# Gates and the first norm's sums by quarters of the tokens in column groups, in place of a gate tile and one running sum

## The chip, the cores and the metric

The kernel runs on one core of a Trainium2 chip. The metric is device time in microseconds, the median of the runs shown. TensorE (PE in the profile) multiplies, VectorE (DVE), ScalarE (ACT) and GpSimd (POOL) do the elementwise work, and SyncE (SP) issues nearly all transfers.

## The reference, cut to what matters

One layer of a hybrid decoder: 576 tokens (512 of a prompt, 64 samples), model width 2048. What this change touches is the first norm, the gates taken from its output, and the softplus and sigmoid of those gates.

```python
h = _rmsnorm(x, norm_mix_g)                    # x * rsqrt(mean(x*x) + EPS) * g
proj = jnp.einsum('bld,de->ble', h, w_in)      # q, k, v, z, gates b and a, mLSTM q, k, v, o, gates i and f
...
beta = jax.nn.sigmoid(dn_b)
g = -jnp.exp(dn_A_log) * jax.nn.softplus(dn_a + dn_dt_bias)
o_dn, S_new = _gated_delta_rule(dq, dkk, dvv, g, beta, S0)
...
ig = ml_i + ml_i_bias
logf = jax.nn.log_sigmoid(ml_f + ml_f_bias)
h_ml, C_new, n_new, m_new = _mlstm(mq, mk, mv, ig, logf, C0, n0, m0)
```

The rest (two head mixers, the output projection, a convolutional feed-forward, a last norm) is the same before and after.

## The kernel before

Everything is held transposed: 128 rows of features by 576 tokens (NT), in two halves of 288 columns (HALF). The width of 2048 makes KT = 16 row tiles of x. A product is done in three parts (high x high, high x low, low x high) with a high and a low half of each operand. For x these are the tiles `ah` and `al`: ACT writes x times the norm's weights g rounded (line 356), DVE the remainder (line 357). For the weights they are `wh` and `wl`: a unit of 128x1024 (`raw`, 512 KB) is loaded by `load_unit`, cast by ACT (line 120) and split by DVE (line 121). Two units make one *tile* of 128 output features: `dense` runs 16 steps of k over it, six products of 288 columns each (line 198). Its result stands in PSUM as a `pd`, of which there are two, so tile n+2 can't begin before tile n has been read out. Single banks of PSUM are called `pr`; there are four.

The norm's factor `rstd` is not applied to x but where a tile is read out of PSUM: `conv_in` (lines 536 to 538) multiplies by it.

PE's order is written out by hand. `tick` is called after each step of k; it lets jobs (generators started by `spawn`) put their own products in between, and `yield n` means n steps of k later. The orders of the other engines are made by a scheduler that follows priorities. At most 23 buffers of 576 columns (`r`) are alive, and a unit of weights has two buffers of each kind (`raw`, `wh`, `wl`).

The start goes like this. `startup` loads x and two units, makes `ah` and `al`, squares x on ACT (line 363) and adds the squares in two running sums, the even ones on DVE and the odd ones on POOL (line 365), joined at line 366. `gates` runs the first tile of w_in, the *gate tile*, whose 128 features hold 24 gates in four groups (0 to 7, 32 to 39, 64 to 67, 96 to 99), the rest zeros; its result lies in two `pr`. `gate_rows` is a job: after 14 steps it sums over the 128 rows with two products of ones (line 256, called from `rms_bc`), makes `rstd`, and then the gates, sigmoid and softplus on all 576 columns (lines 414 to 446). Thirty steps later come the running sums and maxima of the gates, thirty more later their transposes (line 514). After that job the eight delta heads (`dn_head`, each waiting for the gates and for the head two before it) and four mLSTM heads put their products among the tiles. Each head makes the inverse of a triangular matrix in `inverse`; line 843 is the first product of that. `YZ` is how many steps more the inverse of head 0 waits.

Of the kernel before, what the change touches and what calls it, by code (L numbers as in the profile page):

```python
# [36 lines left out]
SEVEN = (1, 0, 2)  # L37
OPA = 1600
YI = 8
YZ = 5  # L40
YS = 11
YJ = 20

# [15 lines left out]
NIN = len(IN_ORDER)  # L59
NR = 23  # L60
NPL = 3
KB1 = 5
YP = 14
H0 = 320
# [4 lines left out]
class Layer:  # L69
# [76 lines left out]
        return self.units.pop(0)  # L146

    def plain_weights(self):
        for name, n in (("w_in", NIN), ("w_out", KT), ("w_up", 2 * NPL - 2)):
            for t in range(n):  # L150
                for u in range(2):
                    yield self.I[name][t][u], False
        for u in range(2):
            for t in range(2):
                yield self.I["w_up"][2 * NPL - 2 + t][u], False

# [127 lines left out]
    def mixer(self):  # L284
        nc, I, O = self.nc, self.I, self.O
        V, A, Pl = nc.vector, nc.scalar, nc.gpsimd
        self.startup()
        jobs = [self.gates()]
        rv = self.v2(self.rstd)
        for h in range(DNH):  # L290
            q, k, v = (self.conv_in(8 * i + h, self.dense()) for i in range(3))
            pd = self.dense()
            sz = self.r()
            with self.urgent():
                V.scalar_tensor_tensor(out=self.v2(sz), in0=self.halves(pd), scalar=0.5, in1=rv, op0=ALU.mult, op1=ALU.mult)
# [36 lines left out]
    def startup(self):  # L332
        nc, I = self.nc, self.I
        self.par = self.cp.tile([P, NPAR], F32, tag="par", name="par")
        nc.gpsimd.dma_start(out=self.par, in_=I["par"])
        self.ones = self.cp.tile([P, P], F32, tag="ones", name="ones")
        nc.vector.memset(self.ones, 1.0)
        self.eps6 = self.cp.tile([P, 1], F32, tag="eps6", name="eps6")
        nc.vector.memset(self.eps6, EPS)
        self.epsh = self.cp.tile([P, 1], F32, tag="epsh", name="epsh")  # L340
        nc.vector.memset(self.epsh, EPS * EPS * P)
        self.rstd = self.cp.tile([P, NT], F32, tag="rstd", name="rstd")

        self.xh, self.xl = [], []
        acc = [self.r(), self.r()]
        xs = []
        acts = [self.new_act(k) for k in reversed(range(KT))][::-1]
        for k in range(KT):
            x = self.r()
            xs.append(x)  # L350
            nc.sync.dma_start(out=x, in_=I["xT"][k])
            if k in (1, 3):
                self.load_unit()
            hi, lo = acts[k]
            g = self.par[:, G1 + k:G1 + k + 1]
            nc.scalar.activation(hi, x, AF.Copy, scale=g)
            nc.vector.scalar_tensor_tensor(out=lo, in0=x, scalar=g, in1=hi.bitcast(F32), op0=ALU.mult, op1=ALU.subtract)
            self.xh.append(hi)
            self.xl.append(lo)
        for k in range(KT):  # L360
            e = nc.gpsimd if k % 2 else nc.vector
            sq = acc[k] if k < 2 else self.r()
            nc.scalar.activation(sq, xs[k], AF.Square)
            if k > 1:
                e.tensor_tensor(out=acc[k % 2], in0=acc[k % 2], in1=sq, op=ALU.add)
        nc.vector.tensor_tensor(out=acc[0], in0=acc[0], in1=acc[1], op=ALU.add)
        self.acc = acc


    def gates(self):  # L370
        nc, I, O = self.nc, self.I, self.O
        V, A, Pl = nc.vector, nc.scalar, nc.gpsimd
        self.con = self.p1.tile([P, NCON], F32, tag="con", name="con")
        Pl.dma_start(out=self.con, in_=I["con"])
        self.ident = self.con[:, C_ID:C_ID + P]
        self.dnst = self.p1.tile([P, 24, 9, 3], F32, tag="dnst", name="dnst")
        Pl.dma_start(out=self.dnst, in_=I["dn_conv"])
        self.cwh = self.p1.tile([P, 96], F32, tag="cwh", name="cwh")
        Pl.tensor_scalar(out=self.cwh, in0=self.par[:, CW:CW + 96], scalar1=0.5, scalar2=None, op0=ALU.mult)
        self.mgh = self.p1.tile([P, 8], F32, tag="mgh", name="mgh")  # L380
# [18 lines left out]
        self.vas = self.p1.tile([64, 257], F32, tag="vas", name="vas")  # L399
        Pl.memset(self.vas[:, 256:257], 1.0)  # L400

        outs = [self.psr()[:, 0:HALF] for _ in range(2)]
        self.dense(outs)
        return self.spawn(self.gate_rows(outs))

    def gate_rows(self, outs):
        nc, I, O = self.nc, self.I, self.O
        V, A, Pl = nc.vector, nc.scalar, nc.gpsimd
        yield 14
        self.rms_bc(self.acc[0], self.rstd)  # L410
        gr = self.r()
        for hf in range(2):
            sl = slice(hf * HALF, (hf + 1) * HALF)
            V.tensor_tensor(out=gr[:, sl], in0=outs[hf], in1=self.rstd[:, sl], op=ALU.mult)
        yield 6
        edge = self.tc.issue_after(self.last_evac.ins)
        edge.__enter__()
        y = self.r()
        V.tensor_scalar(out=y, in0=gr, scalar1=self.par[:, GB:GB + 1], scalar2=self.con[:, C_SG:C_SG + 1], op0=ALU.add, op1=ALU.mult)
        R1, R2, R3 = self.r(), self.r(), self.r()  # L420
        for t in (R1, R2, R3):
            Pl.memset(t, 0.0)
        th = self.r()
        A.activation(th[0:8], gr[0:8], AF.Tanh, scale=0.5)
        V.tensor_scalar(out=R1[0:8], in0=th[0:8], scalar1=0.5, scalar2=0.5, op0=ALU.mult, op1=ALU.add)

        e = self.r()
        A.activation(e, y, AF.Abs)
        A.activation(e, e, AF.Exp, scale=-1.0)
        d = self.r()  # L430
        V.tensor_scalar(out=d, in0=e, scalar1=2.0, scalar2=None, op0=ALU.add)
        V.reciprocal(d, d)
        V.tensor_tensor(out=e, in0=e, in1=d, op=ALU.mult)
        V.tensor_tensor(out=d, in0=e, in1=e, op=ALU.mult)
        p = self.r()
        V.tensor_scalar(out=p, in0=d, scalar1=1.0 / 17, scalar2=None, op0=ALU.mult)
        for c in (15, 13, 11, 9, 7, 5, 3):
            V.scalar_tensor_tensor(out=p, in0=p, scalar=1.0 / c, in1=d, op0=ALU.add, op1=ALU.mult)
        V.scalar_tensor_tensor(out=e, in0=p, scalar=1.0, in1=e, op0=ALU.add, op1=ALU.mult)
        sp = self.r()  # L440
        V.tensor_scalar(out=sp, in0=y, scalar1=0.0, scalar2=None, op0=ALU.max)
        V.scalar_tensor_tensor(out=sp, in0=e, scalar=2.0, in1=sp, op0=ALU.mult, op1=ALU.add)
        coef = self.sm(1, "coef", 1)
        A.activation(coef, self.par[:, AL:AL + 1], AF.Exp)
        V.tensor_scalar(out=coef, in0=coef, scalar1=-1.0, scalar2=None, op0=ALU.mult)
        V.tensor_scalar(out=sp, in0=sp, scalar1=coef, scalar2=None, op0=ALU.mult)
        edge.__exit__(None, None, None)
        yield 30
        edge = self.tc.issue_after(self.last_evac.ins)
        edge.__enter__()  # L450
        rm = self.r()
# [53 lines left out]
        yield 30  # L505
# [1154 lines left out]
```

## Time and profile before

| | |
|---|---|
| Median of 3 runs | 2697.01 us (2695.82 to 2698.49) |
| Profiled execution, its own time | 2699.44 us |
| its span | 2697.7 us |
| TensorE busy | 98% of the span |
| VectorE busy | 74% |
| ScalarE busy | 40% |
| GpSimd busy | 12% |
| Granted TensorE clock, mean | 0.995 |

TensorE's share leaves 46.7 us of the span in which it does nothing. A row of the order of time names start, duration, engine, line, operation and tiles, how many in a row were merged (xN), and in brackets how long the engine was idle before and what released it. Records of matmuls overlap, so their spacing tells the price and not their length. A plain product of 32-bit operands leaves two records.

### The profile page before, as it was taken

The numbers are of one execution on the slowest core, as the hardware profiler recorded it, in microseconds if no ns is written. First come the engines' busy times: TensorE is split into PE (matmuls) and PEld (weight loads), VectorE is DVE, ScalarE is ACT, GpSimd is POOL, SyncE is SP. The second block draws the span as 40 slices with busy tenths as digits, with TensorE's granted clock in tenths as the row PEclk, the third lists the DMA queues.
The fourth block names the chain that finished last, engine by engine and source line by source line (L and its number), as shares of the span: only waits on it lengthen the run. The fifth ranks groups of instructions, "written<-read, shape, count | busy, mean of one in ns | idle before, by whom it ended". The sixth has DMA issues, their size and how long they took to land.

```text
span 2697.7 us, 48872 instructions
## 1 busy us (share of the span) xinstructions
PE 2651.0 (98%) x19967; PEld 2607.0 (97%) x19967; DVE 1994.0 (74%) x3338; ACT 1080.2 (40%) x1704; POOL 333.6 (12%) x658
## 2 busy tenths in 40 slices
PE   7999999999999999998999999999999999999998
PEld 7998999999999999998999999999999999999998
DVE  7887777765544332389888888888888888888646
ACT  5334344443333322254444444444444433433324
POOL 3222322222211001101000000000000100000001
PEclk9999999999999999999999999999999999999999
DMA  5222222222333344444333333333333373342333
GB/s 195 85 77 87 90 91 91 91 88 92 114 113 104 115 135 135 135 123 150 107 111 108 108 108 108 108 108 108 108 108 109 109 256 94 106 146 71 122 97 100
DMA packets 112233, 304.02 MB, mean 113 GB/s; under 512 B 21912, under 2 KB 28184, under 8 KB 112008
## 3 DMA queue, kind: packets, MB, share of 16 engines
q1 hardware_dynamic: 107896, 291.17, 34.0%
q0 software_dynamic: 1872, 7.37, 0.8%
q8 instruction: 156, 2.56, 0.4%
q10 hardware_dynamic: 2240, 2.36, 0.3%
q14 instruction: 69, 0.57, 0.1%
HBM read 264.79 MB, written 36.06 MB: 112 GB/s over the span
## 4 chain that ended last, share of the span: by engine, by line
PE 89%; DVE 4%; DMA 1%; issue 0%; ACT 0%; POOL 0%; DVEq 0%; POOLq 0%; SPq 0%; ACTq 0%
PE pd L198 36%; PE pr L1283 31%; PE pd L1283 12%; PE pr L198 3%; PE pr L1509 1%; DVE bl L121 1%; DVE wl L121 1%; DMA r<-hid 0%; DVE r L1544 0%; PE pr L256 0%; PE pr L843 0%; PE pr L980 0%; PE pr L982 0%; PE pr L690 0%; PE pr L687 0%
## 5 line engine op out<-in xcount | busy, mean ns | idle before, releaser
L120 ACT CAST wh<-raw 128x1024 fp32r<-128x1024 f32 (+1 forms) x394 | 404.6, 1027 | 741.1 <-PE pd L198 400.2
L1283 PE MATMUL pr<-bh,wh 128*128 128x288 f32 x2120 | 626.8, 296 | 1.9 <-ACT bh L120 1.9
L1283 PE MATMUL pr<-bh,wl 128*128 128x288 f32 x2120 | 624.6, 295 | 0.5 <-DVE wl L121 0.5
L1283 PE MATMUL pr<-bl,wh 128*128 128x288 f32 x2120 | 624.3, 294 | 0.6 <-DVE bl L121 0.6
L121 DVE TENSOR_TENSOR wl<-raw,wh 128x1024 fp32r<-128x1024 f32 (+1 forms) x394 | 476.5, 1210 | 178.8 <-ACT wh L120 172.4
L198 PE MATMUL pd<-ah,wh 128*128 128x288 f32 x2496 | 560.3, 306 | 0.0
L198 PE MATMUL pd<-ah,wl 128*128 128x288 f32 x2496 | 534.5, 296 | 0.2 <-DVE wl L121 0.2
L198 PE MATMUL pd<-al,wh 128*128 128x288 f32 x2496 | 533.8, 296 | 0.0
L198 PEld LDWEIGHTS pd<-ah,wh 128*128 128x128 f32 x2496 | 401.0, 189 | 14.2 <-issue 7.7
L198 PEld LDWEIGHTS pd<-ah,wl 128*128 128x128 f32 x2496 | 401.8, 189 | 0.5 <-DVE wl L121 0.5
L198 PEld LDWEIGHTS pd<-al,wh 128*128 128x128 f32 x2496 | 401.7, 189 | 0.0
L1283 PEld LDWEIGHTS pr<-bl,wh 128*128 128x128 f32 x2120 | 400.0, 189 | 1.1 <-DVE bl L121 1.1
L1283 PEld LDWEIGHTS pr<-bh,wh 128*128 128x128 f32 x2120 | 398.4, 188 | 2.1 <-ACT bh L120 2.1
L1283 PEld LDWEIGHTS pr<-bh,wl 128*128 128x128 f32 x2120 | 398.9, 188 | 1.2 <-DVE wl L121 1.2
L120 ACT CAST wh<-s 128x1024 fp32r<-128x1024 f32 (+1 forms) x171 | 169.6, 992 | 361.2 <-DVE s L1248 142.2
L1283 PE MATMUL pd<-bh,wh 128*128 128x288 f32 x848 | 252.2, 297 | 5.6 <-ACT wh L120 5.6
L1283 PE MATMUL pd<-bh,wl 128*128 128x288 f32 x848 | 250.8, 296 | 1.7 <-DVE wl L121 1.7
L1283 PE MATMUL pd<-bl,wh 128*128 128x288 f32 x848 | 249.7, 294 | 0.0
L121 DVE TENSOR_TENSOR wl<-s,wh 128x1024 fp32r<-128x1024 f32 (+1 forms) x171 | 196.5, 1149 | 26.0 <-ACT wh L120 18.4
L1283 PEld LDWEIGHTS pd<-bh,wh 128*128 128x128 f32 x848 | 160.3, 189 | 6.1 <-ACT wh L120 6.1
L1283 PEld LDWEIGHTS pd<-bh,wl 128*128 128x128 f32 x848 | 160.6, 189 | 2.2 <-DVE wl L121 2.2
L1283 PEld LDWEIGHTS pd<-bl,wh 128*128 128x128 f32 x848 | 161.0, 190 | 0.0
(400 smaller groups left out, 3501.1 us busy)
## 6 DMA issues: line engine op xcount, KB each, us to landing
raw<-in_w_up SPq DMA_DIRECT2D x176, 512.0 KB
raw<-in_w_in SPq DMA_DIRECT2D x114, 512.0 KB
raw<-in_w_down SPq DMA_DIRECT2D x40, 512.0 KB
raw<-in_w_out SPq DMA_DIRECT2D x32, 512.0 KB
raw<-in_w_down SPq DMA_DIRECT2D x40, 384.0 KB
hid<-r SPq DMA_DIRECT2D x44, 288.0 KB
r<-hid SPq DMA_DIRECT2D x40, 288.0 KB
r<-in_xT SPq DMA_DIRECT2D x32, 288.0 KB
```

Source lines behind the costliest of these rows:

```text
L120: nc.scalar.copy(hi, src)
L121: nc.vector.tensor_tensor(out=lo, in0=src, in1=hi.bitcast(F32), op=ALU.subtract)
L198: mm(outs[hf], w, x[:, hf * HALF:(hf + 1) * HALF], start=first and i == 0, stop=last and i == 2)
L1283: mm(out, w[:, ks], x[:, sl], start=k == 0 and i == 0, stop=k == nk - 1 and i == 2)
L1509: mm(pr[:, 0:n], w[:, ks], acts[kk][:, a * NT + sl.start:a * NT + sl.stop], start=kk == 0 and i == 0, stop=kk == FB - 1 and i == 2)
```

## The change

- **No gate tile.** `plain_weights` begins w_in at tile 1. Of the gate tile's weights only the 8 columns of each of the 4 groups are used (`gate_weights`): four loads of 256 KB, and four GpSimd operations that multiply them by g into `gw`, 32 columns for each k.
- **Gates in column groups.** `gate_rows` puts 16 x 4 plain products among the second tile's steps (after 20 + 1 steps in all): for each k and each quarter of the tokens (144 columns) 32 output rows, each quarter in its own 32 partitions of one bank.
- **Sums in column groups.** Then x is squared in place, odd k on DVE, even k on ACT, and five steps later 16 x 4 products with 32 columns of ones add the squares up over all k, again one quarter of the tokens in each 32 partitions. The two running sums are gone.
- **rstd** is made on 144 columns, one row of each quarter is copied into a row of `wide`, which is zero elsewhere, and five steps later two products of ones spread it over 128 rows and all tokens.
- **Softplus and sigmoid** run on 128 x 144 in place of 128 x 576; 24 steps later two products with `there` bring the results back to one row per gate.
- **The first tile leaves PSUM raw**: ACT copies it into an `r`, and `rstd` is applied to the copy.
- **The first transfers**: the first unit comes ahead of x, the second after x 7, the third after x 14; of `par` only the 16 columns of g are loaded first; par, con and dnst move from GpSimd's queue to SP's, behind x.
- **Products of ones**: 14 products of 128 columns at the very start, that nothing reads.
- `YZ` is 10 in place of 5.

```diff
-YZ = 5
+YZ = 10
...
+NW = 14
...
-        for name, n in (("w_in", NIN), ("w_out", KT), ("w_up", 2 * NPL - 2)):
-            for t in range(n):
+        for name, t0, n in (("w_in", 1, NIN), ("w_out", 0, KT), ("w_up", 0, 2 * NPL - 2)):
+            for t in range(t0, n):
...
-            q, k, v = (self.conv_in(8 * i + h, self.dense()) for i in range(3))
+            if h == 0:
+                q0, pd = self.r(shape=[P, 2, HALF]), self.dense()
+                A.copy(q0, self.halves(pd))
+                pd = self.dense()
+                q, k = self.conv_in(0, q0), self.conv_in(8, pd)
...
-        nc.gpsimd.dma_start(out=self.par, in_=I["par"])
+        g1 = self.r(shape=[P, KT])
+        nc.gpsimd.dma_start(out=g1, in_=I["par"][:, G1:G1 + KT])
...
+        pw = self.psr()
+        for _ in range(NW):
+            nc.tensor.matmul(pw[:, 0:P], self.ones, self.ones, start=True, stop=True)
...
         for k in range(KT):
+            if k in (0, 8, 15):
+                self.load_unit()
             x = self.r()
             nc.sync.dma_start(out=x, in_=I["xT"][k])
-            if k in (1, 3):
-                self.load_unit()
...
-        for k in range(KT):
-            e = nc.gpsimd if k % 2 else nc.vector
-            sq = acc[k] if k < 2 else self.r()
-            nc.scalar.activation(sq, xs[k], AF.Square)
-            if k > 1:
-                e.tensor_tensor(out=acc[k % 2], in0=acc[k % 2], in1=sq, op=ALU.add)
-        nc.vector.tensor_tensor(out=acc[0], in0=acc[0], in1=acc[1], op=ALU.add)
+        for k in range(0, KT, 4):
+            self.gate_weights(k, g1)
+        nc.sync.dma_start(out=self.par, in_=I["par"])
...
-        outs = [self.psr()[:, 0:HALF] for _ in range(2)]
-        self.dense(outs)
...
-        yield 14
-        self.rms_bc(self.acc[0], self.rstd)
+        Q = NT // 4
+        quarters = [(slice(32 * j, 32 * j + 32), slice(Q * j, Q * j + Q)) for j in range(4)]
+        yield 20
+        for k in range(KT):
+            for s, t in quarters:
+                mm(pg[s], self.gw[:, k], self.xs[k][:, t], start=k == 0, stop=k == KT - 1)
+            if k % 2:
+                V.tensor_tensor(out=self.xs[k], in0=self.xs[k], in1=self.xs[k], op=ALU.mult)
+            else:
+                A.activation(self.xs[k], self.xs[k], AF.Square)
+        yield 5
+        ps = self.psr()[:, 0:Q]
+        for k in range(KT):
+            for s, t in quarters:
+                mm(ps[s], self.ones[:, 0:32], self.xs[k][:, t], start=k == 0, stop=k == KT - 1)
+        rq, wide = self.r(shape=[P, 3, Q]), self.r()
+        self.rsqrt_bc([(ps, slice(0, Q))], 1.0 / D, self.eps6, EPS, rq[:, 0], rq[:, 1], rq[:, 2])
+        for j, (s, t) in enumerate(quarters):
+            (A.copy if j % 2 else V.tensor_copy)(wide[32 * j:32 * j + 1, t], rq[32 * j:32 * j + 1, 0])
...
+        yield 5
+        for sl in halves:
+            mm(pr, self.ones, wide[:, sl], start=True, stop=True)
+            A.copy(self.rstd[:, sl], pr)
```

What moves on the engines is seen at three places. First TensorE in the second real tile; `x4` is one quad. Before, the two products of ones stand there, on the joined sums `r_91`:

```order
L198 MATMUL pd_388<-ah_95,wh_336 128x288 x2
L198 MATMUL pd_388<-al_96,wh_336 128x288 x2
L198 MATMUL pd_388<-ah_95,wl_337 128x288 x2
L256 MATMUL pr_491<-r_91,ones 128x288
L256 MATMUL pr_493<-r_91,ones 128x288
L198 MATMUL pd_388<-ah_93,wh_336 128x288 x2
```

After, the first quads of the gates (`r_107` is gw, `r_146` and so on are x) stand after step 5 of that tile, and those of the sums five steps behind them:

```order
L199 MATMUL pd_373<-ah_130,wh_214 128x288 x2
L199 MATMUL pd_373<-al_131,wh_214 128x288 x2
L199 MATMUL pd_373<-ah_130,wl_215 128x288 x2
L429 MATMUL pr_275<-r_146,r_107 32x144 x4
L429 MATMUL pr_275<-r_150,r_107 32x144 x4
```

```order
L199 MATMUL pd_373<-ah_120,wl_321 128x288 x2
L438 MATMUL pr_526<-r_146,ones 32x144 x4
L438 MATMUL pr_526<-r_150,ones 32x144 x4
L438 MATMUL pr_526<-r_154,ones 32x144 x4
```

The two products on one joined sum have become 32 quads on sixteen tiles each, in two blocks.

Second, VectorE behind the last low halves `al`. Before:

```order
L357 SCALAR_TENSOR_TENSOR al_94<-r_197,par,ah_93 128x576
L365 TENSOR_TENSOR r_91<-r_91,r_203 128x576
L121 TENSOR_TENSOR wl_283<-raw_280,wh_282 128x1024
L121 TENSOR_TENSOR wl_337<-raw_334,wh_336 128x1024
L365 TENSOR_TENSOR r_91<-r_91,r_209 128x576
L365 TENSOR_TENSOR r_91<-r_91,r_215 128x576
```

After:

```order
L122 TENSOR_TENSOR wl_215<-raw_212,wh_214 128x1024
L368 SCALAR_TENSOR_TENSOR al_109<-r_218,r_83,ah_108 128x576
L431 TENSOR_TENSOR r_150<-r_150 128x576
L431 TENSOR_TENSOR r_158<-r_158 128x576
L431 TENSOR_TENSOR r_166<-r_166 128x576
L122 TENSOR_TENSOR wl_321<-raw_318,wh_320 128x1024
```

The adds have become squares in place, and the split for the second tile stands ahead of the last low half.

Third, VectorE at the end of the softplus, in the changed kernel alone; line 494 writes what the products with `there` read, and `wl_859` is the split of a unit for tile 5:

```order
L489 SCALAR_TENSOR_TENSOR r_725<-r_725 128x144
L603 SCALAR_TENSOR_TENSOR r_847<-r_840,cwh,r_847 128x600
L492 SCALAR_TENSOR_TENSOR r_724<-r_725,cq_722,r_724 128x144
L122 TENSOR_TENSOR wl_859<-raw_856,wh_858 128x1024
L494 SCALAR_TENSOR_TENSOR r_726<-r_724,cq_722 32x144 x4
```

The last four steps of the softplus stand behind that split.

## Rows read from the trace of the kernel before

**Rows 1.** The page, section 1: busy time and share of the span by engine.
```profile
PE 2651.0 (98%) x19967; PEld 2607.0 (97%) x19967; DVE 1994.0 (74%) x3338; ACT 1080.2 (40%) x1704; POOL 333.6 (12%) x658
```

**Rows 2.** Who PE waited for: sum in us, times, longest.
```profile
PE pr L843 <- DVE r L836: 3.1, 1, 3.1
PE pr L657 <- DVE r L628: 1.9, 2, 1.5
```

**Rows 3.** Order of time, 0 to 26 us: start, length, engine, line, operation.
```profile
3.67 1.28 ACT L356 ACT_TABLE_LOAD   x1 [3.67 <-DMA r<-in_xT]
...
9.31 1.04 ACT L120 CAST wh<-raw 128x1024 fp32r<-128x1024 f32 x1 [2.52 <-DMA raw<-in_w_in]
...
10.41 0.85 PE L198 MATMUL pr<-ah,wh 128*128 128x288 f32 x2 [10.41 <-ACT wh L120]
...
12.82 0.68 PE L198 MATMUL pr<-al,wh 128*128 128x288 f32 x2
...
13.30 0.66 PE L198 MATMUL pr<-ah,wl 128*128 128x288 f32 x2
...
14.75 8.10 DVE L357 SCALAR_TENSOR_TENSOR al<-r,par,ah 128x576 fp32r<-128x576 f32 x11
...
25.04 0.42 PE L198 MATMUL pd<-ah,wh 128*128 128x288 f32 x2
```

**Rows 4.** Stretches of 2 us: busy by engine, clock, DMA share, GB/s.
```profile
2.00:4.00 2.00, 0.00 (x0) 0.00 (x0) 0.00 (x0) 0.33 (x1) 1.02 (x2) 1.00 0.92 336
...
22.00:24.00 2.00, 2.00 (x18) 2.00 (x17) 1.68 (x4) 2.00 (x4) 0.00 (x0) 1.00 1.02 414
```

**Rows 5.** Order of time, 28 to 49 us, around the sum of squares.
```profile
28.20 9.63 DVE L365 TENSOR_TENSOR r<-r,r 128x576 f32<-128x576 f32 x5
...
36.73 0.42 PE L198 MATMUL pd<-al,wh 128*128 128x288 f32 x2
36.99 0.42 PE L198 MATMUL pd<-ah,wl 128*128 128x288 f32 x2
41.76 2.29 PE L256 MATMUL pr<-r,ones 128*128 128x288 f32 x4 [4.35 <-DVE r L366]
...
48.07 0.43 PE L198 MATMUL pd<-ah,wh 128*128 128x288 f32 x2
```

**Rows 6.** A stretch of 2 us behind the sum; the clock stands third from the end.
```profile
42.00:44.00 2.00, 2.00 (x5) 1.43 (x6) 0.35 (x1) 0.50 (x1) 0.00 (x0) 0.50 0.41 160
```

**Rows 7.** Order of time, PE at 1165 us: products of ones at the full clock.
```profile
1164.98 1.13 PE L256 MATMUL pr<-r,ones 128*128 128x288 f32 x4
...
1166.21 0.42 PE L198 MATMUL pd<-al,wh 128*128 128x288 f32 x2
```

**Rows 8.** Order of time, PE: eight products in column groups, twice, and their neighbours.
```profile
179.51 0.42 PE L198 MATMUL pd<-ah,wl 128*128 128x288 f32 x2
179.86 0.65 PE L747 MATMUL pr<-st,kqs 128*32 128x128 f32 x16
180.43 0.53 PE L198 MATMUL pd<-ah,wh 128*128 128x288 f32 x2
...
651.59 0.39 PE L771 MATMUL pr<-vm,kp 96*128 96x512 f32 x1
651.91 1.07 PE L1004 MATMUL pr<-st,qim 128*32 128x257 f32 x16
652.92 0.53 PE L198 MATMUL pd<-ah,wh 128*128 128x288 f32 x2
```

**Rows 9.** Groups by line, DVE from 44 to 100 us: busy us, mean ns.
```profile
L121 DVE TENSOR_TENSOR wl<-raw,wh 128x1024 fp32r<-128x1024 f32 x9 | 11.0, 1220 | 4.7 <-ACT wh L120 4.4
L545 DVE SCALAR_TENSOR_TENSOR r<-r,cwh,r 128x600 f32<-128x600 f32 x9 | 7.6, 839 | 0.1
L438 DVE SCALAR_TENSOR_TENSOR r<-r,r 128x576 f32<-128x576 f32 x7 | 5.2, 749 | 0.0
```

**Rows 10.** The stretch of heads 0 to 3: busy by engine, clock, DMA.
```profile
110.00:320.00 210.00, 202.86 (x1588) 192.39 (x1587) 154.14 (x389) 88.08 (x217) 66.06 (x90) 1.00 0.26 82
```

More of the change, by code (lines that the diff above doesn't have):

```diff
@@ L290, in mixer @@
         for h in range(DNH):
-            q, k, v = (self.conv_in(8 * i + h, self.dense()) for i in range(3))
+            if h == 0:
[4 more added lines that the diff above has]
+            else:
+                q, k = (self.conv_in(8 * i + h, self.dense()) for i in range(2))
+            v = self.conv_in(16 + h, self.dense())
             pd = self.dense()
@@ L342, in startup @@
         self.rstd = self.cp.tile([P, NT], F32, tag="rstd", name="rstd")
-        self.xh, self.xl = [], []
-        acc = [self.r(), self.r()]
-        xs = []
+        pw = self.psr()
+        for _ in range(NW):
+            nc.tensor.matmul(pw[:, 0:P], self.ones, self.ones, start=True, stop=True)
+        self.xh, self.xl, self.xs = [], [], []
+        self.gw = self.r(shape=[P, KT, 32])
         acts = [self.new_act(k) for k in reversed(range(KT))][::-1]
         for k in range(KT):
+            if k in (0, 8, 15):
+                self.load_unit()
             x = self.r()
-            xs.append(x)
+            self.xs.append(x)
             nc.sync.dma_start(out=x, in_=I["xT"][k])
-            if k in (1, 3):
-                self.load_unit()
             hi, lo = acts[k]
-            g = self.par[:, G1 + k:G1 + k + 1]
+            g = g1[:, k:k + 1]
             nc.scalar.activation(hi, x, AF.Copy, scale=g)
@@ L359, in startup, with gate_weights @@
             self.xl.append(lo)
-        for k in range(KT):
-            e = nc.gpsimd if k % 2 else nc.vector
-            sq = acc[k] if k < 2 else self.r()
-            nc.scalar.activation(sq, xs[k], AF.Square)
-            if k > 1:
-                e.tensor_tensor(out=acc[k % 2], in0=acc[k % 2], in1=sq, op=ALU.add)
-        nc.vector.tensor_tensor(out=acc[0], in0=acc[0], in1=acc[1], op=ALU.add)
-        self.acc = acc
+        for k in range(0, KT, 4):
+            self.gate_weights(k, g1)
+        nc.sync.dma_start(out=self.par, in_=I["par"])
+    def gate_weights(self, k, g1):
+        raw = self.r(shape=[P, 4, 4, 32])
+        self.nc.sync.dma_start(out=raw, in_=self.I["w_in"][0][k // 8][:, k % 8 * P:(k % 8 + 4) * P].rearrange("p (k g w) -> p k g w", k=4, g=4))
+        self.nc.gpsimd.tensor_tensor(out=self.gw[:, k:k + 4].rearrange("p k (g w) -> p k g w", g=4), in0=raw[:, :, :, 0:8],
+                                     in1=g1[:, k:k + 4].unsqueeze(2).unsqueeze(3).to_broadcast([P, 4, 4, 8]), op=ALU.mult)
     def gates(self):
@@ L373, in gates @@
         self.con = self.p1.tile([P, NCON], F32, tag="con", name="con")
-        Pl.dma_start(out=self.con, in_=I["con"])
+        nc.sync.dma_start(out=self.con, in_=I["con"])
         self.ident = self.con[:, C_ID:C_ID + P]
         self.dnst = self.p1.tile([P, 24, 9, 3], F32, tag="dnst", name="dnst")
-        Pl.dma_start(out=self.dnst, in_=I["dn_conv"])
+        nc.sync.dma_start(out=self.dnst, in_=I["dn_conv"])
         self.cwh = self.p1.tile([P, 96], F32, tag="cwh", name="cwh")
@@ L400, in gates, with gate_rows @@
         Pl.memset(self.vas[:, 256:257], 1.0)
-        outs = [self.psr()[:, 0:HALF] for _ in range(2)]
-        self.dense(outs)
-        return self.spawn(self.gate_rows(outs))
-    def gate_rows(self, outs):
+        return self.spawn(self.gate_rows())
+    def gate_rows(self):
         nc, I, O = self.nc, self.I, self.O
-        V, A, Pl = nc.vector, nc.scalar, nc.gpsimd
-        yield 14
-        self.rms_bc(self.acc[0], self.rstd)
[L411 to L415, printed above, removed]
+        V, A, Pl, mm = nc.vector, nc.scalar, nc.gpsimd, nc.tensor.matmul
+        Q = NT // 4
+        quarters = [(slice(32 * j, 32 * j + 32), slice(Q * j, Q * j + Q)) for j in range(4)]
+        halves = [slice(hf * HALF, (hf + 1) * HALF) for hf in range(2)]
+        pg = self.psr()[:, 0:Q]
+        yield 20
[4 more added lines that the diff above has]
+                V.tensor_tensor(out=self.xs[k], in0=self.xs[k], in1=self.xs[k], op=ALU.mult)
+            else:
+                A.activation(self.xs[k], self.xs[k], AF.Square)
[5 more added lines that the diff above has]
+        rq, wide = self.r(shape=[P, 3, Q]), self.r()
+        Pl.memset(wide, 0.0)
+        self.rsqrt_bc([(ps, slice(0, Q))], 1.0 / D, self.eps6, EPS, rq[:, 0], rq[:, 1], rq[:, 2])
+        for j, (s, t) in enumerate(quarters):
+            (A.copy if j % 2 else V.tensor_copy)(wide[32 * j:32 * j + 1, t], rq[32 * j:32 * j + 1, 0])
+        there, back = self.r(shape=[P, 4, 32]), self.r(shape=[P, 4, 4, 8])
+        cs = self.r(shape=[P, 6])
+        for t in (there, back, cs[:, 3:6]):
+            Pl.memset(t, 0.0)
+        for j, (s, _) in enumerate(quarters):
+            Pl.tensor_copy(there[s, :, 0:8], self.ident[s, s].rearrange("p (g w) -> p g w", g=4))
+            Pl.tensor_copy(back[s, :, j], self.ident[s, 32 * j:32 * j + 8].unsqueeze(1).to_broadcast([32, 4, 8]))
+            n, v = ((3, 0.5), (5, 1.0), (4, 1.0), (5, 1.0))[j]
+            Pl.memset(cs[s, n:n + 1], v)
+        Pl.tensor_copy(cs[:, 0:2], self.par[:, GB:GB + 2])
+        Pl.tensor_copy(cs[:, 2:3], self.con[:, C_SG:C_SG + 1])
+        yield 5
+        for sl in halves:
+            pr = self.psr()[:, 0:HALF]
+            mm(pr, self.ones, wide[:, sl], start=True, stop=True)
+            A.copy(self.rstd[:, sl], pr)
+        yield 4
+        pc = self.psr()
+        mm(pc[:, 0:6], back.rearrange("p j g w -> p (j g w)"), cs, start=True, stop=True)
+        cq = self.sm(7, "cq", 1)
+        A.copy(cq[:, 0:6], pc[:, 0:6])
@@ L416, in gate_rows @@
         edge = self.tc.issue_after(self.last_evac.ins)
         edge.__enter__()
[L418 to L425, printed above, removed]
@@ L427, in gate_rows @@
-        e = self.r()
+        c = lambda i: cq[:, i:i + 1]
+        gr, t4, t5 = self.r(shape=[P, 3, Q]), self.r(shape=[P, 3, Q]), self.r()
+        gr, y, val = (gr[:, i] for i in range(3))
+        e, d, p = (t4[:, i] for i in range(3))
+        V.tensor_tensor(out=gr, in0=pg, in1=rq[:, 0], op=ALU.mult)
+        V.tensor_scalar(out=y, in0=gr, scalar1=c(0), scalar2=c(2), op0=ALU.add, op1=ALU.mult)
+        Pl.memset(t5, 0.0)
+        A.activation(val, gr, AF.Tanh, scale=0.5)
+        V.tensor_scalar(out=val, in0=val, scalar1=c(3), scalar2=c(3), op0=ALU.mult, op1=ALU.add)
@@ L428, in gate_rows @@
         A.activation(e, y, AF.Abs)
         A.activation(e, e, AF.Exp, scale=-1.0)
-        d = self.r()
         V.tensor_scalar(out=d, in0=e, scalar1=2.0, scalar2=None, op0=ALU.add)
@@ L434, in gate_rows @@
         V.tensor_tensor(out=d, in0=e, in1=e, op=ALU.mult)
-        p = self.r()
         V.tensor_scalar(out=p, in0=d, scalar1=1.0 / 17, scalar2=None, op0=ALU.mult)
-        for c in (15, 13, 11, 9, 7, 5, 3):
-            V.scalar_tensor_tensor(out=p, in0=p, scalar=1.0 / c, in1=d, op0=ALU.add, op1=ALU.mult)
+        for n in (15, 13, 11, 9, 7, 5, 3):
+            V.scalar_tensor_tensor(out=p, in0=p, scalar=1.0 / n, in1=d, op0=ALU.add, op1=ALU.mult)
         V.scalar_tensor_tensor(out=e, in0=p, scalar=1.0, in1=e, op0=ALU.add, op1=ALU.mult)
[L440 to L446, printed above, removed]
-        edge.__exit__(None, None, None)
-        yield 30
+        V.tensor_scalar(out=d, in0=y, scalar1=0.0, scalar2=None, op0=ALU.max)
+        V.scalar_tensor_tensor(out=d, in0=e, scalar=2.0, in1=d, op0=ALU.mult, op1=ALU.add)
+        A.activation(c(6), c(1), AF.Exp)
+        V.tensor_scalar(out=c(6), in0=c(6), scalar1=c(5), scalar2=-1.0, op0=ALU.mult, op1=ALU.mult)
+        V.scalar_tensor_tensor(out=val, in0=d, scalar=c(6), in1=val, op0=ALU.mult, op1=ALU.add)
+        for s, t in quarters:
+            V.scalar_tensor_tensor(out=t5[s, t], in0=y[s], scalar=cq[s, 4:5], in1=val[s], op0=ALU.mult, op1=ALU.add)
+        edge.__exit__(None, None, None)
+        yield 24
+        R1, R2, R3 = self.r(), self.r(), self.r()
+        for t in (R1, R2, R3):
+            Pl.memset(t, 0.0)
+        sp = y = self.r()
+        for sl in halves:
+            pr = self.psr()[:, 0:HALF]
+            mm(pr, there.rearrange("p g w -> p (g w)"), t5[:, sl], start=True, stop=True)
+            A.copy(sp[:, sl], pr)
+        A.copy(R1[0:8], sp[0:8])
+        yield 5
         edge = self.tc.issue_after(self.last_evac.ins)
@@ L504, in gate_rows @@
         edge.__exit__(None, None, None)
-        yield 30
+        yield 26
         nc.sync.dma_start(out=self.rowd[0:8], in_=G[32:40])
```

## Prediction

> **What bounds the kernel now.** I read section 1 of the page first, then who TensorE waited for, then the first 50 us in order of time on PE, DVE and ACT, then the few stretches where a row prices a new operation. TensorE is busy for 2651.0 of 2697.7 us [rows 1], so an edit is worth what it takes out of TensorE's own list, or out of the gaps in it. Of the gaps the two longest that this change touches are the start, 10.4 us [rows 3], and 4.35 us before the sum of squares [rows 5]; a third, 3.1 us at line 843, lies in a head whose place the change moves [rows 2], in a stretch where all gaps sum to 7.1 us (202.86 busy of 210) [rows 10]. The reader should see in the start that PE waits for the cast of the first weights, and the cast for their transfer, not for x [rows 3]; and at the sum that DVE adds squares from 28.20 on, each add nearly twice its usual length, while PE has nothing left in front of the two products of ones [rows 5].
>
> **Prices.** Two products of 288 columns (a pair) take 0.26 us at the full clock (36.73 to 36.99 [rows 5]); one step of k is three pairs, 0.79 us, and a tile of 16 steps 12.6 us. The same 94 real tiles stand in both kernels, so I count only what is not one of them.
>
> **Before, up to 48 us.** The gate tile ends, and the first real tile begins, at 25.04 [rows 3]; the next weights then cost about 0.4 us more. From the last pair before the sum, which ends at 37.25 (36.99 + 0.26), to 48.07, where the clock is back, 10.8 us pass [rows 5] and nine pairs are done in them (2.3 us): 8.5 us lost. Of this 4.35 is the gap, and the rest are the products of ones and the pairs behind them, which run while the granted clock is 0.50, that is 1.2 GHz [rows 6]; what came ahead of the fall was that idle gap. Together 25.0 + 0.4 + 8.5 = 33.9 us.
>
> **After: the first tile.** The first weights are now the first transfer, and par, con and dnst (1.0 MB) no longer run beside it. The first transfer landed at 3.67, and 0.34 MB/us flowed then [rows 3, 4]; 0.5 MB should land at about 4.0. A table load (1.28) and a cast (1.04) follow [rows 3]: 6.3 us. From there the longest list is DVE's: three splits at 1.14 (1.22 less the 0.08 by which the next one overlaps [rows 9]) and sixteen low halves at 0.736 (8.10/11 [rows 3]), 15.2 us, so the last low half is there at 21.5 and the tile ends two pairs later, at 22.1. x is not the limit: 16 tiles of x and three units of weights are 6.3 MB, at 0.34 and later 0.41 MB/us [rows 4] all there by about 19. The fourteen products of ones run while PE has nothing to do and cost nothing; without them the first pairs would stand 0.48 us apart as before (12.82 to 13.30 [rows 3]), but DVE sets the pace, so they are worth 1.5 us at most. In excess of one tile: 22.1 - 12.6 = 9.5 us.
>
> **After: products in column groups.** The gates and the sums are 16 quads each, four products of 32 rows by 144 columns in four column groups. The nearest rows are two pairs of quads: 8 products of 128 columns occupy PE from 179.77 (179.51 and its pair) to 180.43, 0.66 us; 8 of 257 columns from 651.91 to 652.92, 1.01 us [rows 8]. If the four went one after another, a full product of 288 columns taking 0.485 (below), eight of 257 would need 3.5 us: they run together. Columns are worth 0.485/288 us each, so 144 are worth 0.24. A quad of 128 took 0.33 where its columns are worth 0.22; one of 257 took 0.56, counted from the end of the product before it (651.59 and 0.23 for its 512 columns at 0.13 per 288, so 651.8), where they are worth 0.43. Some 0.12 us a quad is over in both. If that is the entering and leaving of the column groups, paid once a block, a block is 16 x 0.24 + 0.25 = 4.1 us; if it is paid at every quad, 16 x 0.36 = 5.8. I take 4.5, nearer the lower end, because both rows have dense products on either side, so entering and leaving is in them. Two blocks: 9.0 us (8.2 to 11.6).
>
> The Trainium skill ("TensorE: Matmul & The Clock Gate", Part 3, Measured speedup vs the span model) has three column groups together 2.38 times as fast as alone, 0.79 a group. By that a quad would cost 0.30 us and a block 4.9, 0.8 us more for both blocks; the rows here lie within its reach.
>
> **After: broadcasts.** Two times two full-width products of 288 columns (rstd, and the rows of the gates): a pair took 1164.98 to 1166.21 less the dense pair in it, 0.97 us [rows 7]; 1.9 us for both, and 0.2 for the small product of 6 columns.
>
> **After: where chains must arrive.** (1) The gate weights: their four transfers and con and par stand behind x on SP, 8.0 MB in all, at 23 us; POOL's four short products by the norm's weights follow (no row prices them; by 24 to 25.5); PE wants them at 22.1 + 5 steps = 26.0. Next on SP stand dnst and the second half of tile 2's weights, 8.9 MB, at 25.5, and these are wanted at step 8, after the gates, near 33. (2) The squares: eight on DVE and eight on ACT at 0.75 follow their gate product each (from 26.3), with one split and one cast between: done at 34. The first sum stands five steps after the gates, at 34.5, the last square is wanted at 38.5. (3) rstd: sums end at 39.0, five steps on, at 42.9, PE wants the wide row. Between lie an activation, four short DVE steps and copies of 144 columns, 2 to 2.5 us. All three are covered; the raw first tile lets tile 3 start without rstd. (4) The softplus ends in a product after step 11 of tile 4. Counted from there, PE gets to it at 22.1 + 43 steps (33.8) + 9.0 + 1.2 = 66.1. DVE is full from rstd (44.0) on: 9 convolution steps at 0.76, 3 splits at 1.14, 20 steps of 144 columns at about 0.25 (a third of 0.75) [rows 9] and some 12 evacuations and short steps, 5.4 us: 20.7, then a split that can't start before tile 4's step 8 (64.9 at best, with its cast) and four short steps: 67.0. So a wait of **1.0 us** (0 to 3).
>
> Sum: 9.5 + 9.0 + 1.9 + 0.2 + 1.0 = 21.6 us against 33.9: 12.3 us less. Heads 0 and 2 stand 14 steps later against the real tiles, heads 1 and 3 to 7 as before. The 3.1 us at line 843 [rows 2] came where the tail of head 1 met the serial steps of head 2 on DVE; that tail now lies 14 steps earlier against head 2, but heads 2 and 3 are 45 steps apart instead of 59. I count zero, from -5 to +4. **Forecast: 12 us less.** The profiled execution took 2699.4 us with a span of 2697.7; I expect about 2685.7 as the span, and from the median of 2697.0 a time of **2685.0 us**, 2680.5 to 2689.5 with the bounds above.
>
> **Rivals.** (A) New waits eat a third to a half: DVE from 44 to 67 us is booked without a gap, so any delay of rstd passes to the softplus and to PE one for one, and two heads close together add a wait like that of 3.1 us. Plus 5 to 8 us: 2690 to 2693. For it: DVE's list. Against: that list was longer before, a softplus step taking 0.75 us rather than about 0.25 [rows 9]. (B) The records, not the columns, set the pace of a block. Products of this type leave two records each; the sixteen of 257 columns stand 63 ns apart [rows 8]. At that pace 128 records take 8.1 us, two blocks 7.2 us more than I count: 2692. Against: sixteen of 128 columns stood 36 to 41 ns apart. The Trainium skill (same page, Part 1, "Wait — 56ns, not 53.3ns?") has about 62 ns per product where the sequencer's own code decodes them, a bound once the array needs less than that; the 128-column rows speak against it here. (C) **Slower:** in a long block the groups run one after another, each accumulating onto its own part of one bank; the rows that I go by are two quads long and accumulate nothing. 64 products at 0.24 are 15.4 us, 10.9 more per block and 21.8 in all: 2706.8. It turns slower from 10.5 us a block on. Against: rows 8. (D) More gain: the head's 3.1 us and its smaller neighbours go: 2680. That the change doesn't do what it says (PE's list stays as long) is excluded: 96 products of the gate tile are gone from its order.
>
> **Chances.** Forecast 0.61, A 0.17, B 0.06, C 0.07, D 0.09. What can be told from no change is about 0.2%, 5.4 us, so faster means under 2691.6: the forecast, D and two thirds of A, 0.81; the rest of A and B 0.12; slower 0.07. The range from 2679 to 2692.5 leaves out C, and the ends of A and D.
>
> **What would show it.** First product of a real tile at 6.5 to 8 us and the second tile at 21.5 to 23; blocks of 4 to 5.8 us; no gap over 1 us ahead of the sums and the wide row; granted clock 1.00 from 10 to 100 us; a short wait at the product of the softplus rows. A block of over 8 us, a clock of 0.50 behind one, or gaps in heads 0 to 3 that sum to over 12 us (7.1 before) make it wrong.

## The result and the profile after

The kernel before took 2697.17 us (median of 15 executions, 2694.2 to 2700.0), the changed one 2703.28 us (15 executions, 2700.3 to 2706.7): a ratio of 1.0022, 95% interval 1.0014 to 1.0030. It is 6 us slower where 12 us less were forecast. The profiled execution has a span of 2699.9 us (2697.7 before) and took 2701.72 us. In one run below, e14, the profiled execution ran at a mean granted clock of 0.65 and took 3666.7 us, so its trace is not read and its time is that of the other eleven. Section 1 of the page, which answers to [rows 1]:

```profile
PE 2653.2 (98%) x20161; PEld 2608.5 (97%) x20161; DVE 1981.7 (73%) x3340; ACT 1073.9 (40%) x1700; POOL 329.4 (12%) x672
```

The first 70 us in order of time (start, length, engine, line, operation, in brackets the wait), to be held against [rows 3, 5]:

```profile
0.74 1.28 ACT L121 ACT_TABLE_LOAD   x1 [0.74 <-PEq L1694]
...
4.44 1.04 ACT L121 CAST wh<-raw 128x1024 fp32r<-128x1024 f32 x1 [2.42 <-DMA raw<-in_w_in]
...
6.85 0.51 PE L199 MATMUL pd<-ah,wh 128*128 128x288 f32 x2
...
22.79 0.54 PE L199 MATMUL pd<-al,wh 128*128 128x288 f32 x2 [0.85 <-DVE al L368]
...
23.43 0.42 PE L199 MATMUL pd<-ah,wh 128*128 128x288 f32 x2
...
27.50 4.13 PE L429 MATMUL pr<-r,r 128*32 128x144 f32 x128
31.56 0.53 PE L199 MATMUL pd<-ah,wh 128*128 128x288 f32 x2
...
35.74 4.13 PE L438 MATMUL pr<-r,ones 128*32 128x144 f32 x128
39.80 0.53 PE L199 MATMUL pd<-ah,wh 128*128 128x288 f32 x2
...
43.88 1.13 PE L459 MATMUL pr<-r,ones 128*128 128x288 f32 x4
...
69.32 1.44 PE L503 MATMUL pr<-r,r 128*128 128x288 f32 x4 [1.72 <-DVE r L494]
```

The start did what it should. The second tile begins at 23.43, each block in column groups takes 4.06 us with no gap ahead of it, nor is there one ahead of the wide row. Excess 23.43 - 12.6 = 10.8, blocks 8.1, broadcasts 2.1, the wait at L503 1.7: 22.7 us against 33.9, so some 11 us were gained by 70 us. The first pair of the fifth real tile, before and then after, shows 10.3:

```profile
84.86 0.43 PE L198 MATMUL pd<-ah,wh 128*128 128x288 f32 x2
```

```profile
74.57 0.43 PE L199 MATMUL pd<-ah,wh 128*128 128x288 f32 x2
```

They are given back behind that, most of them between 110 and 300 us: the 31st tile begins at 533.09 us, 2.6 us later than in the kernel before (530.54). Whom PE waited for from 60 to 700 us (sum, times, longest), against [rows 2]:

```profile
PE pr L901 <- issue: 8.8, 1, 8.8
PE pr L720 <- DVE r L686: 4.0, 2, 2.4
PE pr L503 <- DVE r L494: 1.7, 1, 1.7
```

and stretches (length, busy time of PE, PEld, DVE, ACT, POOL, granted clock, DMA share, GB/s), of the kernel before and then of the changed one:

```profile
110.00:300.00 190.00, 183.24 (x1440) 174.15 (x1438) 138.33 (x339) 77.30 (x180) 56.44 (x77) 1.00 0.27 84
```

```profile
110.00:300.00 190.00, 173.12 (x1329) 165.23 (x1328) 135.12 (x327) 72.21 (x179) 61.50 (x77) 0.97 0.25 78
...
270.00:300.00 30.00, 21.16 (x155) 20.19 (x154) 15.46 (x39) 7.82 (x17) 4.01 (x5) 0.89 0.17 51
...
283.00:285.00 2.00, 1.78 (x9) 1.81 (x9) 0.12 (x1) 0.00 (x0) 0.00 (x0) 0.50 0.00 0
```

Gaps of 16.9 us stand there instead of 6.8. The largest is at L901 (L843 before), the first product of the inverse of head 2. Its chain in order of time, over DVE, SP's queue and PE:

```profile
260.18 0.28 DVE L867 TENSOR_SCALAR r<-r 40x256 f32<-40x256 f32 x1
...
261.17 0.76 DVE L249 SCALAR_TENSOR_TENSOR r<-r,r 128x576 f32<-128x576 f32 x1
...
262.62 0.80 DVE L768 SCALAR_TENSOR_TENSOR r<-r,par,r 128x576 f32<-128x576 f32 x1
...
277.02 0.17 DVE L875 TENSOR_TENSOR r<-r 40x14 f32<-40x14 f32 x1
...
277.22 0.30 SPq L876 DMA_DIRECT2D xd<-r  x1
...
281.68 0.69 DVE L892 TENSOR_TENSOR r<-cx,con 128x512 f32<-128x512 f32 x1 [4.49 <-DMA cx<-xd]
...
283.22 2.05 PE L901 MATMUL pr<-r,r 128*128 128x128 f32 x8 [8.77 <-issue]
284.92 0.83 PE L199 MATMUL pd<-ah,wh 128*128 128x288 f32 x2
```

The serial steps (L867 to the last L875) take 17.0 us here, and among them stand L248, L249 and L768 of the tail of head 1 (L246 to L249 and L768, 3.9 us in all). Then come the way to DRAM and back and the transpose, and only then PE, 8.8 us late; behind the gap the first two pairs stand 0.63 us apart, and the granted clock from 283 to 285 us is 0.50. Before, the serial steps took 13.9 us and the tail began as they ended:

```profile
250.51 0.28 DVE L809 TENSOR_SCALAR r<-r 40x256 f32<-40x256 f32 x1
...
264.19 0.17 DVE L817 TENSOR_TENSOR r<-r 40x14 f32<-40x14 f32 x1
264.28 0.81 DVE L245 TENSOR_SCALAR r<-pr 128x288 f32<-128x288 f32 x2
...
271.21 1.16 PE L843 MATMUL pr<-r,r 128*128 128x128 f32 x8 [3.11 <-DVE r L836]
```

### The profile page after: what moved, and what is told of

Same layout as the page of the kernel before. It is cut to its first block, busy times and chain, and to the rows that moved or that the text cites. A ratio compares the mean times of both kernels' runs of the same rounds, so it can differ in the third digit from the quotient of the medians.

```text
span 2699.9 us, 49301 instructions
## 1 busy us (share of the span) xinstructions
PE 2653.2 (98%) x20161; PEld 2608.5 (97%) x20161; DVE 1981.7 (73%) x3340; ACT 1073.9 (40%) x1700; POOL 329.4 (12%) x672
## 4 chain that ended last, share of the span: by engine, by line
PE 91%; DVE 5%; DMA 1%; issue 1%; ACT 1%; POOL 0%; SPq 0%; DVEq 0%; POOLq 0%; ACTq 0%
PE pd L199 38%; PE pr L1341 31%; PE pd L1341 12%; PE pr L199 3%; PE pr L1567 1%; DVE wl L122 1%; DMA r<-hid 1%; DVE bl L122 1%; DMA r<-in_xT 0%; PE pr L257 0%; DVE r L1602 0%; PE pr L901 0%; PE pr L741 0%; PE pr L745 0%; PE pr L1038 0%
```

## Experiments

Theory H: the start gives what was forecast, and the place of heads 0 and 2, 14 steps later, takes it back. Rival S: the start is worth less than its rows, or costs something later that has nothing to do with the heads. Each ratio is to the kernel before, run on the same chip. "Head 2 later" counts steps of its inverse against the real tiles; gaps are 190 us less PE's busy time from 110 to 300 us; "wait" is that at head 2's first product of the inverse.

| run | head 2 later by | us | ratio (95%) | gaps | wait |
|---|---|---|---|---|---|
| before | 0 | 2697.2 | 1 | 6.8 | 3.1 |
| changed | 14 | 2703.3 | 1.0022 (1.0014 to 1.0030) | 16.9 | 8.8 |
| e1 | 9 | 2702.6 | 1.0014 (1.0005 to 1.0023) | 15.3 | 8.3 |
| e2 | 0 | 2689.1 | 0.9962 (0.9949 to 0.9976) | 5.4 | 1.4 |
| e3, on before | 14 | 2712.3 | 1.0051 (1.0039 to 1.0064) | 17.4 | 10.0 |
| e4 | 14, +12 ahead of the product | 2701.1 | 1.0009 (1.0001 to 1.0018) | 11.3 | 2.8 |
| e5 | 0 | 2684.3 | 0.9948 (0.9936 to 0.9961) | 4.9 | 1.4 |
| e6 | -5 | 2686.2 | 0.9955 (0.9942 to 0.9967) | 4.9 | none |
| e7 | 0 | 2686.4 | 0.9956 (0.9943 to 0.9970) | 5.8 | 1.4 |
| e8 | 5 | 2702.0 | 1.0012 (1.0003 to 1.0021) | 16.4 | 8.6 |
| e9 | 14 | 2702.3 | 1.0012 (1.0003 to 1.0021) | 14.7 | 5.5 |
| e10 | 0 | 2683.9 | 0.9946 (0.9933 to 0.9959) | 4.3 | 0.7 |
| e12 | 16 | 2703.5 | 1.0019 (1.0010 to 1.0028) | 18.0 | 7.2 |
| e14 | 14 | 2693.5 | 0.9981 (0.9972 to 0.9990) | not read | not read |

**Is it the start or the heads?** e1, on the changed kernel:

```
-YZ = 10
+YZ = 5
```

> The changed kernel with YZ back at 5, so that the inverse of head 0, and with it head 2, stands 5 steps earlier and 9 steps later than before instead of 14. Theory H (the start gives its 10 us or so, and heads 0 and 2 that stand 14 steps later, close to heads 1 and 3, take it back in the wait at L901 and the half clock behind it): 2694 to 2700, and L901 of head 2 waits less than 8.8 us. Rival S (the start gives less than its rows say, or costs something later that has nothing to do with the heads): 2703, as the changed kernel.

2702.6 is S's number and outside H's, and the wait is 8.3 us. But e1's eleven executions spread from 2697.7 to 2705.7 us, and four of them lie below all fifteen of the changed kernel. The profiled one is the slowest; it lost 3.6 us more at L503 than the changed kernel's (wait 2.8 us, clock 0.50 from 70 to 76 us). So taking back 5 of the 14 steps leaves most of the loss, and e1 alone doesn't decide. e2 takes back all of them, on the changed kernel:

```
-YZ = 10
+YZ = 5
-        yield 26
+        yield 17
```

> The changed kernel with YZ back at 5 and the last wait of the gate job 17 steps instead of 26: heads 0 and 2 stand where they stood before against the real tiles (14 steps earlier than in the changed kernel), everything in the first 80 us stays. Theory H: gaps of PE between 110 and 300 us fall from 16.8 to about 7, no half clock, 2686 to 2689. Rival S: 2697 or more.

2689.1 us, at the upper end of H's range and 14.2 less than the changed kernel; gaps back to 5.4 us, and the wait at head 2's product is short:

```profile
110.00:300.00 190.00, 184.60 (x1449) 174.64 (x1448) 138.66 (x354) 82.49 (x199) 57.07 (x81) 1.00 0.25 82
...
260.60 1.16 PE L901 MATMUL pr<-r,r 128*128 128x128 f32 x8 [1.44 <-DVE r L894]
```

H holds, and S falls as the account of the loss. e3 makes the same move alone, on the kernel before:

```
-YZ = 5
+YZ = 10
         edge.__exit__(None, None, None)
-        yield 30
+        yield 39
```

> The kernel before with the heads' part of the change alone: YZ 10 and the second wait of 30 steps in the gate job made 39, so that heads 0 and 2 stand 14 steps later, the start untouched. Theory H: a long wait at the first product of head 2's inverse and 9 to 13 us more, 2706 to 2710. Rival S: 2697, within 2 us.

2712.3 us against 2697.85 of before beside it: 14.5 us more, with the start untouched, above what H had priced. PE in order of time:

```profile
291.69 2.04 PE L843 MATMUL pr<-r,r 128*128 128x128 f32 x8 [10.04 <-issue]
```

So the move costs 14.2 and 14.5 us, on either start.

**What the start still lost.** e2's stretches around L503 (columns as above), and its wait there:

```profile
66.00:70.00 4.00, 2.29 (x13) 1.67 (x12) 3.91 (x9) 0.94 (x2) 0.00 (x0) 0.97 0.20 50
70.00:72.00 2.00, 2.00 (x8) 1.71 (x8) 0.95 (x3) 1.04 (x3) 0.00 (x0) 0.50 0.41 162
72.00:74.00 2.00, 2.00 (x13) 2.00 (x13) 1.71 (x3) 1.93 (x4) 0.00 (x0) 0.71 0.05 9
...
69.01 1.99 PE L503 MATMUL pr<-r,r 128*128 128x288 f32 x4 [1.71 <-DVE r L494]
```

A wait of 1.7 us, and the clock at its lower level of 1.2 GHz behind it. e5 is e2 with that product four steps later:

```
-        yield 24
+        yield 28
-        yield 17
+        yield 13
```

> As e2_heads_back (heads 0 and 2 at their old places), and the product of the softplus rows 4 steps (3.2 us) later in PE's order: the wait ahead of it 28 steps instead of 24, the last wait of the gate job 13 instead of 17, so that nothing else moves. If the wait of 1.7 us at that product and the half clock behind it (69.9 to 73.2 us in e2's profile) are what the start still loses, both go and the time is 2684 to 2687. If PE only waits elsewhere for the same DVE list, it stays at 2688 to 2690.

2684.3 us, 4.8 less than e2. In the profiled executions 3.8 of it is there when the fifth tile begins (72.00 us against 75.83): 1.7 is the wait and about 1.7 the clock (8 us at a mean of 0.79 from 66 to 74 in e2). The heads add nothing to it (the 31st tile begins at 516.12 against 520.01); the last 1 us I can't place. The time is the forecast to within 1 us, but with the softplus product moved, which the forecast did not have. The heads alone (e2) leave 2689.1, 4.1 us over the forecast and near the upper end of its range.

e7 is e5 with `NW = 0`, without the products of ones:

> As e5_softplus_later without the fourteen products of ones at the start (NW 0). The prediction priced them at 1.5 us at most, since DVE sets the pace of the first tile: e5 plus 0 to 1.5 us. If the clock of the whole first tile hung on them, e5 plus 4 us or more.

2686.4 us: all five executions lie above all five of e5, by 2.1 us in the median, more than the 1.5 priced. The profiles don't put it at the start: the first pairs run slow (0.48 us apart), but the second tile begins at 22.93 against 23.03 in e5, as DVE and ACT set the pace. About 1 us is a wait at head 0's first product of the inverse (138.02 us) that e5 doesn't have, and the rest arises after 1200 us. Whether the fourteen products have to do with these stays open; in the first tile they gain nothing.

**How the loss grows with the place.** e6 is e5 with `YZ = 0`, e8 is e5 with `YZ = 10`.

> As e5_softplus_later with YZ 0: the inverse of head 0 and all of head 2 five steps earlier than in the kernel before. If the distance between neighbouring heads is what counts, and more is better, the last wait at L901 of head 2 (1.4 us in e2) goes: 2682 to 2686, at or below e5. If it is the exact place of head 2 among the convolution steps of the dense tiles, other waits appear: 2688 or more.

> As e5_softplus_later with YZ 10: the inverse of head 0 and all of head 2 five steps later than in the kernel before (e1 had them 9 later, the changed kernel 14). If the loss grows evenly with the steps, a third of 14 us more than e5: 2689 to 2692. If it sets in with a jump, as e1 (already the whole loss at 9) suggests, it is within 2 us of e5 or at 2696 or more.

e6: 2686.2, just above the first range and below the second. The wait of head 2 is gone and head 0 waits instead (L901, 4.6 us): its own inverse is asked for too soon. e8: 2702.0, a jump of 17.7 us for five steps, with both inverses late:

```profile
148.60 2.08 PE L901 MATMUL pr<-r,r 128*128 128x128 f32 x8 [3.40 <-DVE r L894]
...
275.14 2.08 PE L901 MATMUL pr<-r,r 128*128 128x128 f32 x8 [8.65 <-DVE r L894]
```

**Which part of the chain?** e4 gives head 2 twelve more steps ahead of that product:

```
-        inv = self.inverse(U, res, YZ if h == 0 else 0)
+        inv = self.inverse(U, res, {0: YZ, 2: 12}.get(h, 0))
```

> The changed kernel with 12 steps (9.5 us) more between the diagonal blocks of head 2's inverse and their first product, nothing else moved but head 4, 4 steps later. Theory H in its narrow form (what costs is the one product of PE that is asked for 8.8 us too soon): that gap goes, 2692 to 2695. In its wide form (two heads so close together overfill DVE, whoever waits): the wait comes back at other products of heads 2 and 3, and the time stays over 2699. Rival S: 2703.

The wait falls from 8.8 to 2.8 us, and yet the time only from 2703.3 to 2701.1: the narrow form fails in its number, and the time is that of the wide form. The waits come back not in heads 2 and 3 but further on: head 4, chained to head 2, comes four steps later, and PE is busy for 195.9 us from 400 to 600 us where the changed kernel has 198.8 (one wait of 1.8 us is at L901 again). Here room given to a late head was taken from the next one.

e14 leaves the serial loop of head 2 out, so that its diagonal blocks are not inverted:

```
-        for j in range(SB - 2, 0, -1):
+        for j in range(SB - 2, 0, -1) if steps else ():
```

> The changed kernel with the 28 products and subtractions of the serial loop left out for head 2 alone (its diagonal blocks are then not inverted, so head 2's results are not the reference's); every place in PE's order stays. In the changed kernel this loop runs 17.0 us on DVE between 260.2 and 277.2. Theory H (the chain of head 2's inverse through DVE is what PE waits for at L901): that wait falls from 8.8 us to under 3, the half clock behind it goes, and the time is 2692 to 2697, the waits of heads 0 and 1 and of head 2's first stage staying. If the wait is put down to the wrong engine and only covers another delay of PE: over 2700.

2693.5 us, 9.8 less, within H's range; the waits were not measured. The chain of head 2's inverse is worth about 10 of the 14 us. The edit also takes 28 steps of about 0.2 us each off DVE, so the chain and the load on DVE are not told apart.

e9 moves the tail of head 1 out of those steps, on the changed kernel; e12 is e5 with heads 0 and 2 one whole tile later (`yield 29` for `yield 13`).

```
-        yield 6
+        yield 34 if h == 1 else 6
```

> The changed kernel with the tail of head 1 alone moved: its wait of 6 steps ahead of the last sum is 34, which in DVE's order takes the five steps L246 to L249 and L768 of head 1 (3.9 us) from ahead of and among the serial steps of head 2's inverse to behind the steps that PE waits for at L901. Theory T (the tail of head 1 inside head 2's serial steps is the main cause): the wait of 8.8 us falls by 4 to 6 us, and the time to 2694 to 2699. Theory P (it is the phase: head 2's stand against the evacuation and the convolution steps of the dense tiles, which come every 16 steps): the wait stays at 6 us or more and the time over 2700.

> As e5_softplus_later with the last wait of the gate job 29 instead of 13: heads 0 and 2 stand 16 steps later, exactly one dense tile, so that head 2 meets the convolution steps of the dense tiles as in e5, but the tail of head 1 in its serial steps, 16 steps closer. T: a wait of 5 us or more at L901 and 2695 or more. P: a wait under 3 us and 2684 to 2690.

SP's queue, DVE and PE up to that product in e9, then PE in e12:

```profile
271.88 0.30 SPq L876 DMA_DIRECT2D xd<-r  x1
273.96 0.33 SPq L130 DMA_DIRECT2D raw<-in_w_in  x1
274.38 0.39 SPq L879 DMA_DIRECT2D cx<-xd  x1
...
277.79 0.69 DVE L892 TENSOR_TENSOR r<-cx,con 128x512 f32<-128x512 f32 x1 [3.86 <-DMA cx<-xd]
...
279.33 2.05 PE L901 MATMUL pr<-r,r 128*128 128x128 f32 x8 [5.55 <-issue]
```

```profile
286.32 2.05 PE L901 MATMUL pr<-r,r 128*128 128x128 f32 x8 [7.18 <-DVE r L894]
```

e12 (2703.5) speaks against P: the same phase against the dense tiles, and the wait is there. It is 19.2 us over e5 where e8, 5 steps later, is 17.7 over it: past the jump more steps cost little. e9 bears T out in part only, and its time is the one that P gave. The serial steps shrink to 12.1 us and end 5.3 us earlier, but the wait falls by 3.2 us: a weight load stands between the two transfers on SP's queue, and from issue of the first to the next step on DVE 5.9 us pass instead of 4.5. And the time is 2702.3, 1 us less: the late tail brings new waits (PE busy 98.0 of 300 to 400 us, 99.4 before the edit), and behind the 5.5 us the granted clock is still 0.50 (279 to 283 us).

e10 is e5 with the same wait of head 1 at 14 for 6.

> As e5_softplus_later with the tail of head 1 eight steps later (6 becomes 14), so that in DVE's order it stands behind the serial steps and the transposes of head 2's inverse. By T the last wait at L901 (1.4 us) goes: 2682 to 2684. If the wait moves to the tail's own readers, 2684 to 2686.

2683.9 us: the wait halves to 0.7 us, and the time can't be told from e5's. e5 and e10 beat both kernels, by 0.5% the kernel before. e5's chain (DVE, SP, PE), to be held against that of the changed kernel:

```profile
237.56 0.28 DVE L867 TENSOR_SCALAR r<-r 40x256 f32<-40x256 f32 x1
...
251.25 0.17 DVE L875 TENSOR_TENSOR r<-r 40x14 f32<-40x14 f32 x1
251.34 0.81 DVE L246 TENSOR_SCALAR r<-pr 128x288 f32<-128x288 f32 x2
...
251.44 0.30 SPq L876 DMA_DIRECT2D xd<-r  x1
...
255.14 0.68 DVE L892 TENSOR_TENSOR r<-cx,con 128x512 f32<-128x512 f32 x1
...
256.63 1.16 PE L901 MATMUL pr<-r,r 128*128 128x128 f32 x8 [1.45 <-DVE r L894]
```

## Why the prediction was wrong

- **First tile**: 9.5 us of excess forecast, 10.8 found. DVE's list runs from 5.52 to 22.74, 17.2 us for the 15.2 that I added up: it stands still for 1.6 us, waiting for ACT's casts and high halves, which themselves wait for x and the weights. It begins 0.8 us before the 6.3 that I counted, because the table load (at 0.74) ran while the first transfer was under way and not behind it. The step was right, the term 1.3 us too small.
- **Column groups**: 4.5 us a block forecast (4.1 to 5.8), 4.06 found, just below the lower end: 0.18 us over the 16 x 0.24 of the columns, so what is over at entering and leaving is paid once a block. Rivals B and C fall. The Trainium skill ("TensorE: Matmul & The Clock Gate", Part 3, Measured speedup vs the span model) would have a block at 4.9, an estimate from its figure for three groups; the measurement decides. Its 62 ns per product (Part 1, Wait — 56ns, not 53.3ns?) does not bind if it is meant per record, 128 records in 4.06 us being 32 ns each. Per product they are 63 ns, where the columns alone are worth 61, so nothing here, nor [rows 8] at 41 ns a record, shows whether it binds per product.
- **Broadcasts, chains 1 to 3**: as forecast; no wait ahead of L429, L438 and L459.
- **Softplus**: a wait of 1.0 us forecast (0 to 3), 1.7 found. What I left out is the clock: in the changed kernel's profiled execution it stayed at 1.00 there, but in e2's it fell to 0.50, and e2 and e5 differ by 4.8 us.
- **Heads**: this step failed. "I count zero, from -5 to +4" was +14.2 us (changed kernel less e2), and +14.5 in e3. I had read [rows 2] rightly, the 3.1 us come where the tail of head 1 meets the serial steps of head 2, and had the direction: the tail lies 14 steps earlier against head 2. But I took the tail to leave the steps that way. It had begun at 264.28, as they ended, so that earlier meant into them. I never looked up where in the steps it stood. The runs show in place of the zero a wait of 8.8 us at head 2's first product of the inverse, behind a chain on DVE that is worth 9.8 us (e14).
- **Rival A** named this mechanism (two close heads add a wait like that of 3.1 us) but priced it at one more such wait. What it lacks is the sum: 8.8 instead of 3.1 at one product, two waits of 1.5 us at head 0 (120.41 and 164.97), and the half clock behind the long gap.
- **The test named beforehand**, gaps of over 12 us in heads 0 to 3, showed it: 16.9 us from 110 to 300 alone.
- **The range**: the bounds named for the blocks, the wait and the heads add up to 2678 to 2694, wider than the 2680.5 to 2689.5 that I gave. The measured 2703.3 lies outside both.

Without the heads' move the time is 2689.1 us (e2), within the range; that e5 (2684.3) comes to within 1 us of the forecast of 2685.0 is in part luck, since there the softplus product moved too and its terms miss on both sides (first tile +1.3, blocks -0.9). What stays open: of the loss only the chain is shown (e14: 9.8 us of 14.2), and of the wait itself only the tail's share (e9: 3.2 us of the 7.3 by which changed kernel and e2 differ), which gave back 1 us of time. That the tail is the main cause is not shown. Heads 0 and 2 moved together in e1, e2, e3, e6, e8 and e12, so their shares are not separated. Why DVE also begins the serial steps later after head 2's first product (22.0 us in the changed kernel, 18.1 in e2) was not separated by a run.

## What to carry to other kernels

A step that only moves in the order is not free because it keeps its length: look up, for the engine that is shared, what stands among its serial steps now and what will stand there after the move, and take a place with a wait of a few us for what may be the edge of a jump, as it was here, and not for the middle of a range of both signs. Move one thing at a time: the same start with the heads left alone is 0.4% faster than the kernel before (e2), with them moved 0.2% slower.

## What the runs showed of the hardware

The clock behind a short wait does not follow from the wait's length alone. At L503 a wait of 1.72 us left it at 1.00 (changed kernel), one of 1.71 us was followed by 0.50 (e2), one of 2.8 us by 0.50 for 6 us (e1); the wait of 3.1 us at L843 before left the eight records behind it at 1.16 us, and behind one of 3.4 us in e8 eight records of the same form took 2.08. The Trainium skill ("TensorE: Matmul & The Clock Gate", Part 1, What's actually happening) says that the number of slow products varies from run to run of one kernel; the executions of the changed kernel, 2700.3 us at a mean clock of 0.995 and 2706.7 at 0.993, fit that.
